# A gated-delta-rule scan in a two-layer hybrid kernel, rewritten so that each chunk takes one product and one addition

## The chip, the cores and the metric

The kernel runs on one core of a Trainium2 chip. The metric is the device time of one launch in microseconds (us). PE is TensorE (matrix products), PEld its weight loads, DVE is VectorE, ACT is ScalarE, POOL is GpSimd, SP is SyncE, which only issues DMAs here.

## The reference

There are 1024 tokens of width 1024 and two hybrid layers, followed by a second kind of block that the change doesn't touch. A hybrid layer projects its normed input to many columns, runs three mixers on them (GDN, a gated delta rule with 6 heads of 64; MLA, softmax attention with 6 heads; RWKV, a second recurrence with 4 heads), and projects their joined output back. GDN and RWKV run forwards and backwards over the tokens. GDN works in 16 chunks of 64 tokens; the change concerns its scan over the chunks:

```python
sol = lax.linalg.triangular_solve(a_mat, rhs, left_side=True, lower=True, unit_diagonal=True)
u0, w = sol[..., :dv], sol[..., dv:]
p_intra = jnp.einsum('nhcid,nhcjd->nhcij', q, k) * d_incl
q_g = q * gam[..., None]
k_d = k * jnp.exp(cum[..., -1:] - cum)[..., None]
g_end = jnp.exp(cum[..., -1])

def step(s, inp):
    w_c, u0_c, p_c, qg_c, kd_c, ge_c = inp
    u = u0_c - jnp.einsum('nhcd,nhde->nhce', w_c, s)
    o = jnp.einsum('nhcd,nhde->nhce', qg_c, s) + jnp.einsum('nhij,nhje->nhie', p_c, u)
    s = ge_c[..., None, None] * s + jnp.einsum('nhcd,nhce->nhde', kd_c, u)
    return s, o
```

## The kernel before

A hybrid layer has two stages. Stage A makes the input projection and, woven into it, GDN. Stage B runs MLA and RWKV woven together; after it comes the output projection.

The projections are the line L1036, here called dense: 128x512 products of high and low halves, 48 for an output tile, 27 tiles or 1,296 products in stage A of a layer and 384 for the output. In stage A, `paced` ties every second dense product to a tick on SP behind the products before, so that the scheduler spreads them among GDN's work. A dense product otherwise waits only for its weights (loaded by SP, split into high and low by ACT L996 and POOL L1000).

GDN takes its 6 heads in three pairs (head pairs 0, 1, 2), with the two directions on the two halves of the partitions. `gdn_front` of a pair is a generator in five phases: (1) convolution and norm of k and q on DVE (L192, L194); (2) convolution of v, transposes, decays; (3) the matrix `am` (L307); (4) the inverse of its diagonal blocks "by lanes" (L317, then 60 short DVE instructions L469 and L470), and the queries `q2` scaled by POOL (L327); (5) transposes back (L338, L341), the off-diagonal block (L350 to L361) and the products u (L375) and w (L380), evacuated by ACT (L366). `gdn_scan` then runs over the chunks of the pair. The text calls the scans S0, S1 and S2. In what order phases and scans are written is set by

```python
SEQ_A = "0 0 T3 1 1 1 0 1 S0 T3 2 2 2 1 2 S1 2 S2"
GDN_BUFS = dict(b8=5, b4=14, pad=2, fs=1, fx=2, gt=1, lan=1, xl=1, lt=1)
```

where a digit is the next phase of that pair, T3 three dense tiles, and GDN_BUFS says how many buffers each kind of tile has. `pt`, `am` and `q2` of a pair are the tiles of kind b8: five buffers for nine tiles in a layer. The two tiles of kind pad hold the input of a convolution, and also the factors `eg` by which `q2` is multiplied. `xt` is another name for `am`. Products that aren't dense use three PSUM banks (`k.ps`), the scan one (`k.pss`), its outputs another (`k.pso`).

A step of the scan before has two halves in a row: w times the state (`psw`, L419), subtracted from u by DVE (L421), then kd times u (`psk`, L427), added to the decayed state by two DVE instructions (L431). Each half is four 64x64 products (two heads, two directions).

Engines run their instructions in order; the order is fixed ahead, by a scheduler that looks at dependencies and buffers. In stage B the MLA products (scores L968, sums L921, values L931) are dealt out among RWKV's steps, which the text calls E0 to E3 (early parts), L0 to L3 (late parts) and scans; 1,146 MLA products in a layer.

Of the kernel before, what the change touches and what calls it, by code (L numbers as in the profile page):

```python
# [207 lines left out]
def gdn_front(k, hp, raw, prm, decays, eg_dram):  # L208
# [155 lines left out]

# [3 lines left out]
    last = None  # L368
    for b in range(4):
        pu, pw = (k.ps.tile([128, 512], F32, tag="mm", name=n("ps")) for _ in range(2))  # L370
        for j in range(8):
            nn = b * 8 + j
            for d in range(2):
                h = dh[d]
                nc.tensor.matmul(pu[h, j * 64 : j * 64 + 64], lhsT=xt[h, nn, :], rhs=vt(nn)[h], start=True, stop=True)  # L375
        done(pu, vt, b)
        for j in range(8):
            for d in range(2):
                h, m = dh[d], (b * 8 + j - 2) % 32
                nc.tensor.matmul(pw[h, j * 64 : j * 64 + 64], lhsT=gk(m)[h], rhs=xt[h, m, :], start=True, stop=True)  # L380
        if last is not None:
            done(last, gk, b - 1)
        last = pw
    done(last, gk, 3)
    yield dict(u=vt, wt=gk, kd=kd, pt=pt, qg=q2, ge=ge)


def gdn_scan(k, hp, F, prm, y_out):
# [3 lines left out]
    u, wt, kd, pt, qg, ge = (F[x] for x in ("u", "wt", "kd", "pt", "qg", "ge"))  # L392
    dh = [slice(0, 64), slice(64, 128)]
    z3 = lambda ps: ps[:, 0:128].rearrange("p (z e) -> p z e", e=CH)

    def outputs(d, half):
# [3 lines left out]
        for j in range(8):  # L400
            c = (half ^ d) * 8 + j
            sn = 15 - c if d else c
            for z in range(2):
# [3 lines left out]
                if sn:  # L407
                    nc.tensor.matmul(o, lhsT=wt(nn)[h], rhs=qg[h, z, c * 64 : c * 64 + 64], start=False, stop=True)
# [3 lines left out]
    for s in range(NST):  # L412

        after = (s + 1) % NST
        if s:
            psw = k.pss.tile([128, 512], F32, tag="sc", name=n("psw"))
            for h in dh:
                for z in range(2):
                    nc.tensor.matmul(psw[h, z * 64 : z * 64 + 64], lhsT=wt(2 * after + z)[h], rhs=wt(2 * s + z)[h], start=True, stop=True)  # L419
            x = u(2 * s, 2)  # L420
            nc.vector.tensor_tensor(x, x, z3(psw), op=ALU.subtract)  # L421
        if s < 15:
            psk = k.pss.tile([128, 512], F32, tag="sc", name=n("psk"))
            for h in dh:
                for z in range(2):
                    nn = 2 * s + z
                    nc.tensor.matmul(psk[h, z * 64 : z * 64 + 64], lhsT=kd(nn)[h], rhs=u(nn)[h], start=True, stop=True)  # L427
# [1418 lines left out]
```

## Time and profile before

| | |
|---|---|
| device time, median of 3 runs | 4023.65 us (4023.13 to 4024.43) |
| the profiled execution | 4012.39 us, of which the span is 4010.6 us |
| mean granted clock of PE in it | 0.903 of full speed |
| GDN's stage in layer 0, layer 1 | about 35 to 687 us, 1351 to 1985 us |
| second block, untouched | from about 2640 us |

Times inside the span are counted from its start. Busy shares are averages over the span; PE's busy time counts products that overlap in its pipeline with their full length.

### The profile page before, as it was taken

The numbers are of one execution on the slowest core, as the hardware profiler recorded it, in microseconds if no ns is written. First come the engines' busy times: TensorE is split into PE (matmuls) and PEld (weight loads), VectorE is DVE, ScalarE is ACT, GpSimd is POOL, SyncE is SP. The second block draws the span as 40 slices with busy tenths as digits, with TensorE's granted clock in tenths as the row PEclk, the third lists the DMA queues.
The fourth block names the chain that finished last, engine by engine and source line by source line (L and its number), as shares of the span: only waits on it lengthen the run. The fifth ranks groups of instructions, "written<-read, shape, count | busy, mean of one in ns | idle before, by whom it ended". The sixth has DMA issues, their size and how long they took to land. (4 is left out here: it accounts for less than half of the span.)

```text
span 4010.6 us, 70158 instructions
## 1 busy us (share of the span) xinstructions
PE 3444.1 (86%) x28908; PEld 2699.5 (67%) x28908; DVE 2360.2 (59%) x3270; ACT 1782.2 (44%) x2788; POOL 1373.0 (34%) x1367
## 2 busy tenths in 40 slices
PE   5878798798897877879879889779999998999898
PEld 4656665476675655557547667558898877887686
DVE  6695613866653468662485765358999975323223
ACT  6535236354452454423646445343344347555222
POOL 2432111351522243221244242333333445333361
PEclk9889799789888988889979979879999999999899
DMA  3322112000005232211200000411111111111432
GB/s 111 96 70 69 36 60 71 24 7 4 6 2 200 79 93 64 73 50 49 79 24 7 4 6 13 168 65 41 56 54 49 43 53 48 54 54 43 156 114 71
DMA packets 107073, 237.24 MB, mean 59 GB/s; under 512 B 13896, under 2 KB 16328, under 8 KB 106752
## 3 DMA queue, kind: packets, MB, share of 16 engines
q1 hardware_dynamic: 104000, 226.18, 17.3%
q8 instruction: 228, 3.74, 0.4%
q0 software_dynamic: 1024, 3.41, 0.3%
q10 hardware_dynamic: 1728, 3.15, 0.2%
q14 instruction: 93, 0.76, 0.1%
HBM read 164.17 MB, written 62.23 MB: 56 GB/s over the span
## 5 line engine op out<-in xcount | busy, mean ns | idle before, releaser
L1000 POOL TENSOR_TENSOR wl<-wr,wh 128x512 fp32r<-128x512 f32 x332 | 483.4, 1457 | 1421.8 <-ACT wh L996 1370.2
L1036 PE MATMUL psd<-hh,wh 128*128 128x512 f32 (+2 forms) x2272 | 901.6, 397 | 63.4 <-ACT pad L1425 20.7
L1036 PE MATMUL psd<-hl,wh 128*128 128x512 f32 (+2 forms) x2272 | 892.2, 393 | 41.1 <-DVE hl L1000 23.6
L1036 PE MATMUL psd<-hh,wl 128*128 128x512 f32 (+2 forms) x2272 | 888.8, 392 | 26.4 <-SPq L1092 23.2
L1036 PEld LDWEIGHTS psd<-hh,wh 128*128 128x128 f32 x2272 | 447.9, 197 | 160.3 <-ACT hh L996 23.5
L1036 PEld LDWEIGHTS psd<-hl,wh 128*128 128x128 f32 x2272 | 447.6, 197 | 128.1 <-DVE hl L1000 29.4
L1036 PEld LDWEIGHTS psd<-hh,wl 128*128 128x128 f32 x2272 | 449.1, 198 | 108.4 <-POOL wl L1000 19.1
L996 ACT ACTIVATE wh<-wr 128x512 fp32r<-128x512 f32 x332 | 208.2, 628 | 639.1 <-PE psd L1036 341.0
L1202 DVE SCALAR_TENSOR_TENSOR co<-pad,cw,co 128x1024 f32<-128x1024 f32 x240 | 364.6, 1519 | 5.8
L969 DVE TENSOR_REDUCE m<-pss 128x1 f32<-128x512 f32 x192 | 130.6, 686 | 103.8 <-PE pss L968 103.0
L923 ACT ACTIVATE ph<-ps 128x512 fp32r<-128x512 f32 x192 | 114.3, 595 | 170.9 <-PE pso L931 131.2
L924 DVE TENSOR_TENSOR pl<-ps,ph 128x512 fp32r<-128x512 f32 x192 | 131.7, 686 | 79.3 <-ACT ph L923 77.4
L1036 PE MATMUL psd<-hi,wh 128*128 128x512 f32 x384 | 149.8, 393 | 11.7 <-ACT wh L996 11.7
L973 ACT ACTIVATE p<-pss,m 128x512 f32<-128x512 f32 x192 | 130.0, 683 | 60.2 <-DVE m L970 50.1
L931 PE MATMUL pso<-pl,v 128*64 128x256 f32 x384 | 112.8, 328 | 50.8 <-DVE pl L924 50.4
L1036 PE MATMUL psd<-hi,wl 128*128 128x512 f32 x384 | 149.6, 392 | 5.3 <-POOL wl L1000 5.3
L1036 PE MATMUL psd<-lo,wh 128*128 128x512 f32 x384 | 150.1, 393 | 0.0
L469 POOL TENSOR_TENSOR lt<-lan,xl 64x30 f32<-64x30 f32 (+14 forms) x240 | 143.5, 598 | 17.4
L931 PE MATMUL pso<-ph,v 128*128 128x256 f32 x384 | 135.2, 357 | 16.4 <-ACT ph L923 10.5
L470 POOL TENSOR_TENSOR xl<-xl,lt 64x30 f32<-64x30 f32 (+14 forms) x240 | 142.8, 595 | 18.2
L1036 PE MATMUL psd<-mh,wh 128*128 128x512 f32 x256 | 101.8, 412 | 47.9 <-ACT wh L996 35.2
L921 PE MATMUL ps<-cst,p 128*128 128x128 f32 x768 | 140.5, 307 | 2.5 <-DVE v L904 2.5
(480 smaller groups left out, 7292.3 us busy)
## 6 DMA issues: line engine op xcount, KB each, us to landing
wr<-in_w_in SPq DMA_DIRECT2D x252, 256.0 KB, 2.6
proj<-st SPq DMA_DIRECT2D x108, 256.0 KB, 2.1
pad<-proj SPq DMA_DIRECT2D x32, 512.0 KB, 3.7
wr<-in_w_out SPq DMA_DIRECT2D x48, 256.0 KB, 2.7
y<-yd SPq DMA_DIRECT2D x16, 512.0 KB, 4.7
sg<-proj SPq DMA_DIRECT2D x16, 512.0 KB, 4.1
x<-x SPq DMA_DIRECT2D x16, 512.0 KB, 4.3
eg<-eg SPq DMA_DIRECT2D x24, 256.0 KB, 4.1
```

Of the source, the lines that this page charges most:

```text
L469: eng.tensor_tensor(t, a, b, op=ALU.mult)
L470: eng.tensor_tensor(x[:, j + 1 :, 0:j], x[:, j + 1 :, 0:j], t, op=ALU.subtract)
L921: yield nc.tensor.transpose(ps[:, c : c + 128], p[i][kt // 4][:, (kt % 4) * 128 : (kt % 4) * 128 + 128], k.c("ident"))
L923: nc.scalar.activation(ph, ps, AF.Copy)
L924: nc.vector.tensor_tensor(pl, ps, ph.bitcast(F32), op=ALU.subtract)
L931: yield nc.tensor.matmul(o, lhsT=l, rhs=r[:, c], start=kt + i == 0, stop=kt + i == 8)
L969: nc.vector.reduce_max(m[:, h : h + 1], pss[h], axis=AX.X)
L973: nc.scalar.activation(p[h], pss[h], AF.Exp, bias=m[:, 2:3], scale=SCALE, accum_out=sums[:, t, h : h + 1])
L996: first = nc.scalar.activation(hi, src, AF.Copy)
L1000: e.tensor_tensor(lo, src, hi.bitcast(F32), op=ALU.subtract)
L1036: yield nc.tensor.matmul(ps, lhsT=w(a)(i), rhs=x[b](i)[:, sl], start=i == 0 and a == b, stop=i == 7 and a == 1)
L1202: eng.scalar_tensor_tensor(out, pad[:, j : j + T], w[:, j : j + 1], out, op0=ALU.mult, op1=ALU.add)
```

## The change

Of the reference's step, u is put into the new state, which gives S to M S + C with M = g_end I − kd^T w and C = kd^T u0: both are known ahead of the scan. The output becomes (q_g − p w) S + p u0. So `gdn_front` phase 5 makes w and u with one loop (L373), then in four banks each M (POOL L380 makes g_end I, PE L386 the product, DVE L387 subtracts) and C (PE L386, ACT copy L365), then in four banks the corrected queries (PE L396, DVE L398 subtracts). `gdn_scan` has 14 steps of four products (L431) and one DVE addition (L433). M is written over `am` (`mt = xt`), C over `kd`, and the states grow in place of C. Lines of the changed kernel up to L460 differ from those before; below that they are one less (L1036 becomes L1035).

```diff
@@ -361,37 +361,50 @@
         nc.scalar.activation(xt[96:128, ns, 0:32], pv[96:128], AF.Copy)
 
 
-
     def done(ps, t, b):
         nc.scalar.activation(t(b * 8, 8), ps.rearrange("p (n d) -> p n d", d=CH), AF.Copy)
 
-    last = None
     for b in range(4):
-        pu, pw = (k.ps.tile([128, 512], F32, tag="mm", name=n("ps")) for _ in range(2))
-        for j in range(8):
-            nn = b * 8 + j
-            for d in range(2):
-                h = dh[d]
-                nc.tensor.matmul(pu[h, j * 64 : j * 64 + 64], lhsT=xt[h, nn, :], rhs=vt(nn)[h], start=True, stop=True)
-        done(pu, vt, b)
-        for j in range(8):
-            for d in range(2):
-                h, m = dh[d], (b * 8 + j - 2) % 32
-                nc.tensor.matmul(pw[h, j * 64 : j * 64 + 64], lhsT=gk(m)[h], rhs=xt[h, m, :], start=True, stop=True)
-        if last is not None:
-            done(last, gk, b - 1)
-        last = pw
-    done(last, gk, 3)
-    yield dict(u=vt, wt=gk, kd=kd, pt=pt, qg=q2, ge=ge)
+        for t in (gk, vt):
+            ps = k.ps.tile([128, 512], F32, tag="mm", name=n("ps"))
+            for j in range(8):
+                nn = b * 8 + j
+                for h in dh:
+                    nc.tensor.matmul(ps[h, j * 64 : j * 64 + 64], lhsT=xt[h, nn, :], rhs=t(nn)[h], start=True, stop=True)
+            done(ps, t, b)
+
+
+    mt = xt
+    for b in range(4):
+        ns = slice(b * 8, b * 8 + 8)
+        nc.gpsimd.tensor_tensor(mt[:, ns], k.c("eye2").unsqueeze(1).broadcast_to([128, 8, CH]), b3(ge[:, ns], CH), op=ALU.mult)
+        pm, pc = (k.ps.tile([128, 512], F32, tag="mm", name=n("ps")) for _ in range(2))
+        for ps, l, r in ((pm, gk, kd), (pc, kd, vt)):
+            for j in range(8):
+                nn = b * 8 + j
+                for h in dh:
+                    nc.tensor.matmul(ps[h, j * 64 : j * 64 + 64], lhsT=l(nn)[h], rhs=r(nn)[h], start=True, stop=True)
+        nc.vector.tensor_tensor(mt[:, ns], mt[:, ns], pm.rearrange("p (n d) -> p n d", d=CH), op=ALU.subtract)
+        done(pc, kd, b)
+    for b in range(4):
+        ps = k.ps.tile([128, 2, 4, CH], F32, tag="mm", name=n("ps"))
+        for j in range(4):
+            for z in range(2):
+                for d, h in enumerate(dh):
+                    c = b * 4 + j
+                    nn = 2 * (15 - c if d else c) + z
+                    nc.tensor.matmul(ps[h, z, j], lhsT=gk(nn)[h], rhs=pt[h, nn, :], start=True, stop=True)
+        x = q2[:, :, b * 256 : b * 256 + 256]
+        nc.vector.tensor_tensor(x, x, ps.rearrange("p z c i -> p z (c i)"), op=ALU.subtract)
+    yield dict(u=vt, m=mt, st=kd, pt=pt, qg=q2)
 
 
 def gdn_scan(k, hp, F, prm, y_out):
 
     nc, g = k.nc, k.g
     n = k.name
-    u, wt, kd, pt, qg, ge = (F[x] for x in ("u", "wt", "kd", "pt", "qg", "ge"))
+    u, m, st, pt, qg = (F[x] for x in ("u", "m", "st", "pt", "qg"))
     dh = [slice(0, 64), slice(64, 128)]
-    z3 = lambda ps: ps[:, 0:128].rearrange("p (z e) -> p z e", e=CH)
 
     def outputs(d, half):
 
@@ -405,34 +418,20 @@
                 o = ps[dh[z], j * 64 : j * 64 + 64]
                 nc.tensor.matmul(o, lhsT=u(nn)[h], rhs=pt[h, nn, :], start=True, stop=sn == 0)
                 if sn:
-                    nc.tensor.matmul(o, lhsT=wt(nn)[h], rhs=qg[h, z, c * 64 : c * 64 + 64], start=False, stop=True)
+                    nc.tensor.matmul(o, lhsT=st(nn - 2)[h], rhs=qg[h, z, c * 64 : c * 64 + 64], start=False, stop=True)
         return ps
 
     y = []
-    for s in range(NST):
-
-        after = (s + 1) % NST
-        if s:
-            psw = k.pss.tile([128, 512], F32, tag="sc", name=n("psw"))
+
+    for s in range(1, NST - 1):
+        psk = k.pss.tile([128, 512], F32, tag="sc", name=n("psk"))
+        for z in range(2):
             for h in dh:
-                for z in range(2):
-                    nc.tensor.matmul(psw[h, z * 64 : z * 64 + 64], lhsT=wt(2 * after + z)[h], rhs=wt(2 * s + z)[h], start=True, stop=True)
-            x = u(2 * s, 2)
-            nc.vector.tensor_tensor(x, x, z3(psw), op=ALU.subtract)
-        if s < 15:
-            psk = k.pss.tile([128, 512], F32, tag="sc", name=n("psk"))
-            for h in dh:
-                for z in range(2):
-                    nn = 2 * s + z
-                    nc.tensor.matmul(psk[h, z * 64 : z * 64 + 64], lhsT=kd(nn)[h], rhs=u(nn)[h], start=True, stop=True)
-            if s:
-                for z in range(2):
-                    nn = 2 * s + z
-                    nc.vector.scalar_tensor_tensor(
-                        wt(nn + 2), wt(nn), ge[:, nn : nn + 1], psk[:, z * 64 : z * 64 + 64], op0=ALU.mult, op1=ALU.add)
-            else:
-                nc.vector.tensor_copy(wt(2, 2), z3(psk))
-        if s in (9, 11):
+                nn = 2 * s + z
+                nc.tensor.matmul(psk[h, z * 64 : z * 64 + 64], lhsT=m[h, nn, :], rhs=st(nn - 2)[h], start=True, stop=True)
+        x = st(2 * s, 2)
+        nc.vector.tensor_tensor(x, x, psk[:, 0:128].rearrange("p (z e) -> p z e", e=CH), op=ALU.add)
+        if s in (8, 10):
             y.append(g.tile([128, 512], F32, tag="fx", name=n("y")))
             nc.scalar.activation(y[-1], outputs(len(y) - 1, 0), AF.Copy)
     for d in range(2):
```

Counted over the program, PE has 20,984 products in place of 20,216 (128 more for each of the six head pairs), DVE 3,112 in place of 3,244 instructions, POOL 24 more, ACT 58 more, SP as many as before.

The first place is PE in S0 of layer 0: a step before, with its two sets of products (`psw`, `psk`) and dense (`psd`) and output products (`pso`) between them,

```order
L419 MATMUL psw_1937<-gk_742 64x64 x4
L1036 MATMUL psd_4339<-hl_230,wh_4265 128x512
L1036 MATMUL psd_4339<-hh_229,wl_4266 128x512
L1036 MATMUL psd_4339<-hh_229,wh_4314 128x512
L1036 MATMUL psd_4339<-hl_230,wh_4314 128x512
L427 MATMUL psk_1943<-vt_748,kd_722 64x64 x4
L406 MATMUL pso_2042<-pt_768,vt_748 64x64
L408 MATMUL pso_2042<-q_220_996,gk_742 64x64
```

and a step of the changed kernel there:

```order
L431 MATMUL psk_2150<-kd_722,am_797 64x64 x4
L421 MATMUL pso_2187<-q_220_996,kd_722 64x64
L419 MATMUL pso_2187<-pt_768,vt_748 64x64
L421 MATMUL pso_2187<-q_220_996,kd_722 64x64
L419 MATMUL pso_2187<-pt_768,vt_748 64x64
L1035 MATMUL psd_4669<-hh_229,wl_4596 128x512
L1035 MATMUL psd_4669<-hh_229,wh_4595 128x512
L1035 MATMUL psd_4669<-hl_230,wh_4595 128x512
L1035 MATMUL psd_4669<-hh_229,wl_4596 128x512
L431 MATMUL psk_2156<-kd_722,am_797 64x64 x4
```

Where eight dense products and two sets of scan products made a step, there are now four dense products, four output products and one set.

The second place is DVE in S0 of layer 0. Before, the steps of S0 (`vt`, `gk`), the lane inverse of head pair 1 (`lt`, `xl`) and the convolutions of head pair 2 (`k_404`, `q_405`, from `pad`) alternate:

```order
L470 TENSOR_TENSOR xl_1812<-xl_1812,lt_1875 128x10x21
L421 TENSOR_TENSOR vt_748<-vt_748,psw_1950 128x128
L194 SCALAR_TENSOR_TENSOR q_405_2539<-pad_2550,prm_174,q_405_2539 128x1024
L194 SCALAR_TENSOR_TENSOR k_404_2538<-pad_2540,prm_174,k_404_2538 128x1024
L469 TENSOR_TENSOR lt_1878<-lan_1807,xl_1812 128x198
L431 SCALAR_TENSOR_TENSOR gk_742<-gk_742,ex_699,psk_1956 128x64 x2
L194 SCALAR_TENSOR_TENSOR q_405_2539<-pad_2550,prm_174,q_405_2539 128x1024
L194 SCALAR_TENSOR_TENSOR k_404_2538<-pad_2540,prm_174,k_404_2538 128x1024
L470 TENSOR_TENSOR xl_1812<-xl_1812,lt_1878 128x9x22
L421 TENSOR_TENSOR vt_748<-vt_748,psw_1963 128x128
```

In the changed kernel DVE has the whole lane inverse of pair 1 first, then the subtractions L387 and L398 of pair 0, then 14 additions of S0 in a row; its last two, and the convolutions of pair 2 behind them:

```order
L433 TENSOR_TENSOR kd_723<-kd_723,psk_2276 128x128
L433 TENSOR_TENSOR kd_723<-kd_723,psk_2282 128x128
L438 TENSOR_TENSOR y_2231<-y_2231,pso_2288 128x512
L192 TENSOR_SCALAR k_400_2648<-pad_2650,prm_174 128x1024
L194 SCALAR_TENSOR_TENSOR k_400_2648<-pad_2650,prm_174,k_400_2648 128x1024 x2
L192 TENSOR_SCALAR q_401_2649<-pad_2660,prm_174 128x1024
L438 TENSOR_TENSOR y_2186<-y_2186,pso_2322 128x512
```

`M` in the buffer of `am` lives until S0 ends, so the `q2` of pair 1 has no buffer of kind b8 until then. On POOL its two products with `eg` stand after the four L380 of pair 0, and the tiles of kind pad that hold `eg` come free for the convolutions of pair 2 behind them.

The third place is PE near the end of stage A of layer 0, at the dense product number 1,200 of 1,296. Before, dense products with few others:

```order
L1036 MATMUL psd_5535<-hh_229,wh_5461 128x512
L1036 MATMUL psd_5535<-hl_230,wh_5461 128x512
L877 MATMUL ps_5797<-sq_5794,cst_58 128x512
L1036 MATMUL psd_5535<-hh_229,wl_5462 128x512
L1036 MATMUL psd_5535<-hh_229,wh_5461 128x512
L1036 MATMUL psd_5535<-hl_230,wh_5461 128x512
L1036 MATMUL psd_5535<-hh_229,wl_5462 128x512
L1036 MATMUL psd_5535<-hh_229,wh_5461 128x512
```

In the changed kernel the products of MLA (L930, L967, L920, of lines one less than before) stand among them:

```order
L1035 MATMUL psd_5819<-hl_230,wh_5748 128x512
L1035 MATMUL psd_5819<-hh_229,wl_5749 128x512
L1035 MATMUL psd_5865<-hh_229,wh_5791 128x512
L1035 MATMUL psd_5865<-hl_230,wh_5791 128x512
L930 MATMUL pso_7125<-ph_7175,v_6165 128x256
L1035 MATMUL psd_5865<-hh_229,wl_5792 128x512
L1035 MATMUL psd_5865<-hh_229,wh_5791 128x512
L967 MATMUL pss_7220<-kh_6097,qh_6099 128x512
L967 MATMUL pss_7220<-kl_6098,qh_6099 128x512
L967 MATMUL pss_7220<-kh_6097,ql_6100 128x512
L930 MATMUL pso_7125<-pl_7176,v_6165 64x256
L930 MATMUL pso_7125<-ph_7175,v_6165 128x256
```

Counted in PE's order of layer 0: ahead of the last output of S2 there stood 1,106 dense products and now 882; by the end of the norm that follows it, 1,122 and now 898; at the last dense product 79 products of MLA had been issued and now 406. From there to RWKV's step E3 there stand 1,708 PE instructions and now 1,680. Behind E3 to the end of stage B there were 1,096, 299 of them of MLA, and now 797, none of MLA. In layer 1 at the end of GDN 2,816 dense products of both layers had been issued and now 2,592 of the 2,976; at the last of them 44 products of MLA and now 380.

## Rows read from the trace of the kernel before

**Rows 1.** The page, busy time of each engine, with its share of the span.
```profile
PE 3444.1 (86%) x28908; PEld 2699.5 (67%) x28908; DVE 2360.2 (59%) x3270; ACT 1782.2 (44%) x2788; POOL 1373.0 (34%) x1367
```

**Rows 2.** Stages of layer 0: length, busy time (instructions) by engine, clock, DMA.
```profile
597.00:687.00 90.00, 74.35 (x279) 49.37 (x278) 30.95 (x51) 58.53 (x81) 19.12 (x20) 0.92 0.19 63
687.00:1069.00 382.00, 320.39 (x2593) 229.80 (x2591) 273.92 (x420) 176.01 (x342) 149.71 (x228) 0.81 0.05 17
1069.00:1227.00 158.00, 138.60 (x1803) 110.47 (x1801) 79.06 (x143) 87.05 (x162) 41.80 (x71) 0.89 0.10 35
```

**Rows 3.** Timeline of POOL, layers 0 and 1: start, length, line, operation, [idle before].
```profile
597.30 0.69 POOL L858 DMA_DIRECT2D mc<-cs  x1
...
687.15 0.96 POOL L90 MEMSET rm<- 128x1024 bf16 x1 [13.94 <-PE psd L1036]
...
1922.93 0.56 POOL L858 DMA_DIRECT2D mc<-cs  x1
...
1985.87 0.96 POOL L90 MEMSET rm<- 128x1024 bf16 x1
```

**Rows 4.** Line L1036 alone in stretches of layer 0: PE busy, PEld busy, clock, DMA.
```profile
268.00:374.00 106.00, 54.12 (x176) 33.65 (x174) 0.87 0.24 72
...
489.00:597.00 108.00, 64.47 (x216) 37.62 (x216) 0.98 0.15 50
597.00:655.00 58.00, 33.07 (x111) 22.36 (x109) 0.88 0.26 84
663.00:687.00 24.00, 14.19 (x48) 8.00 (x47) 1.00 0.06 23
```

**Rows 5.** Timeline of PE and DVE, one step of the scan of head pair 2.
```profile
549.27 0.46 PE L419 MATMUL psw<-gk 64*64 64x64 f32 x8
...
549.78 0.29 DVE L421 TENSOR_TENSOR vt<-vt,psw 128x128 f32<-128x128 f32 x1 [1.31 <-PE psw L419]
...
550.22 0.40 PE L1036 MATMUL psd<-hl,wh 128*128 128x512 f32 x1
...
550.45 0.40 PE L1036 MATMUL psd<-hh,wl 128*128 128x512 f32 x1
...
552.56 0.46 PE L419 MATMUL psw<-gk 64*64 64x64 f32 x8
```

**Rows 6.** Timeline of PE, a bank of 64x64 products ahead of the scan.
```profile
276.52 1.10 PE L375 MATMUL ps<-vt,am 64*64 64x64 f32 x32
```

**Rows 7.** Timeline of POOL at head pair 1's queries.
```profile
288.75 4.82 POOL L327 TENSOR_TENSOR q<-q,eg 128x1024 f32<-128x1024 f32 x2 [8.12 <-DMA q<-q]
```

**Rows 8.** Timeline of DVE, layer 0, head pairs 0 to 2.
```profile
280.44 0.21 DVE L469 TENSOR_TENSOR lt<-lan,xl 128x30 f32<-128x30 f32 x1 [0.80 <-ACT xl L462]
...
376.34 0.69 DVE L439 TENSOR_TENSOR y<-y,pso 128x512 f32<-128x512 f32 x1 [2.27 <-PE pso L408]
...
429.53 8.12 DVE L317 STREAM_TRANSPOSE lan<-am 32x1024 f32<-32x1024 f32 x4 [8.92 <-PE ps L358]
438.77 0.20 DVE L469 TENSOR_TENSOR lt<-lan,xl 128x30 f32<-128x30 f32 x1 [1.12 <-ACT xl L462]
...
466.56 2.00 DVE L338 STREAM_TRANSPOSE am<-xl 32x1024 f32<-32x1024 f32 x1
```

**Rows 9.** Timeline of PE, MLA's smaller products in a row.
```profile
700.87 0.40 PE L931 MATMUL pso<-pl,v 128*64 128x256 f32 x2
...
701.23 0.60 PE L921 MATMUL ps<-cst,p 128*128 128x128 f32 x4
```

**Rows 10.** Line L968 alone (MLA's scores) in three stretches.
```profile
597.00:655.00 58.00, 0.00 (x0) 0.12 (x1) 0.88 0.26 84
663.00:687.00 24.00, 5.40 (x19) 3.62 (x20) 1.00 0.06 23
687.00:1069.00 382.00, 69.48 (x192) 37.73 (x191) 0.81 0.05 17
```

**Rows 11.** Timeline of DVE, RWKV's scan with MLA finished.
```profile
1206.29 0.22 DVE L751 TENSOR_TENSOR kb<-kb,psg 128x64 f32<-128x64 f32 x1 [0.58 <-PE psg L750]
```

## The prediction

> **What bounds the kernel now.** I read the page's busy times first, and don't take them as they stand: PE is at 86%, but its weight loads, which run beside the products, are at 67% [rows 1], and in an undisturbed stretch one dense product starts 0.23 us behind the other while each counts 0.40 us [rows 5]. So PE has slack, and the question is which chain holds each stage. The reader takes that from POOL's timeline [rows 3]. MLA's first instruction (L858) is issued at 597.30 in layer 0, when GDN has ended (the end of S2 with its outputs and norm; I read 593). RWKV's first (L90) is issued at 687.15, having waited 13.94 us for a dense product, the last of the 1,296. So there are two gates in a layer: the end of GDN opens MLA, the end of dense opens RWKV. In layer 1 the same two instructions stand at 1922.93 (GDN ends at about 1910) and 1985.87.
>
> Then the stages [rows 2]: 90 us with dense and the start of MLA (597 to 687), 382 us with RWKV and MLA woven (687 to 1069, up to E3), and 158 us behind it. RWKV lies behind the last dense product, so whatever moves that product moves the layer's end, less what RWKV gains by having fewer MLA products among its own.
>
> Dense runs in GDN's shadow: 176 products in 106 us of S0's time, 216 in 108 us of S2's [rows 4]. At 0.23 us each they fill a third to a half of it. GDN's time is thus no pure loss, and a shorter GDN pushes dense out behind it. The order (front part) says by how much: of 1,296 dense products 1,122 stood ahead of the end of GDN, now 898.
>
> **The change part by part.**
>
> *A scan step.* In S2 one step took 3.29 us, from one L419 to the next [rows 5]; the DVE subtraction is 0.29 us, and it had waited 1.31 us. The new step has four dense products (0.92 us) and one set of scan products (0.46 us with its tail): 1.4 us. Fourteen of these are 20 us, where 15 of 3.29 were 49.
>
> *Work added ahead of the scan.* 128 map products, 64 of the queries. A bank of 16 products (32 records) takes 1.10 us [rows 6], of which I count the last 0.17 as pipeline, so 12 banks at 0.93 are 11 us of PE; what the scan loses is 64 of its 124 products, 3.7 us. The net is 7.4 us a pair, 22 us a layer, 44 us in all. Of DVE, eight 128x512 passes out of PSUM; the like L439 takes 0.69 us [rows 8], 5.5 us a pair. The removed are 15 subtractions and 28 short L431, about 12 us. With three PSUM banks for all of this and ACT copies between, u, w, maps and queries of a pair should take about 24 banks x 0.93 = 22 us, less what of them lies inside the phase before.
>
> *The first scan, S0.* The order on DVE puts the maps' last subtractions behind the whole lane inverse of pair 1 (from 280.44; another pair's took 27.8 us, from 438.77 to 466.56), two more subtractions (1.4) and the transposes back (five or six of 2.00 us) [rows 8]: 318 to 320, with the four subtractions of the queries 323. PE has no dense product in its queue there, so it stands still for some 36 us. Then 14 steps, 20 us, and the rest of the outputs, 12 us: S0 ends at about 355, before at 376 [rows 8]. A gain of 21 us.
>
> *The buffer that is held.* M lives in `am`, so the queries of pair 1 wait for S0's end; before they were scaled by POOL at 288.75 [rows 7], 4.82 us for the two, and the `pad` tiles came free for pair 2's convolutions, which DVE did inside S0. Now: DMA of q2 4 us, POOL 4.8, load of pad 3.6, convolutions and norm of k and q 20, v 11, `am` of pair 2 14, then the off-diagonal blocks of pair 1: about 417. The lane transposes of pair 2 stood at 429.53, having waited 8.92 us [rows 8]: 12 of the 21 us are kept. Transposes 8, lane inverse 27.8 as now (438.77 to 466.56 [rows 8]), transposes 11: 466. S1 follows with 21 us, then u to queries of pair 2 (to 512) and S2 with outputs and norm, 30 us: GDN ends at about **543 instead of 593**. I take the same 50 us for layer 1: 1860 instead of 1910. Bounds: 30 if evacuations with three banks are slow, 70 if pair 2's convolutions are not late.
>
> *What then waits.* At 543 there are 398 dense products left, with 406 of MLA among them. MLA needs its start-up first: no score product in the 58 us after 597, with 111 dense [rows 4, 10]. Taken with its loads as 68 us and 152 dense products, that is 611. Then 246 dense products mixed with 366 of MLA, which come in units of 12 L968, 16 L931 and 16 L921 (44). PE alone could do dense and L968 at 0.23 us, L931 at 0.12, L921 at 0.11 [rows 5, 9]: 246 x 0.23 + 366 x 0.145 = 109 us. The only stretch that has both shows 48 dense and 19 L968 (1.6 units) in 24 us [rows 4, 10], 15.2 us a unit; but its L931 lag, and by all three lines there were 1.1 units, 21.6 us each. The 8.3 units are 127 us by the first, 180 by the second. I take 135, nearer to the first, since MLA's softmax has no RWKV beside it. Dense ends at 611 + 135 = 746 instead of 687: **+59**. Layer 1: 384 dense products left at 1860; 68 us; then 232 dense with 346 of MLA, 127 us: 2055 instead of 1985, **+70**.
>
> *What comes back.* From there to E3 PE's order has 28 instructions fewer out of 1,708, and 740 of MLA for 768: the 382 us stay, less 8. Behind E3 no MLA is left, where 299 of it lay before. PE was busy 138.60 of 158 us there [rows 2]; 299 x 0.145 = 43 us of that goes, but the bare chain shows too: a scan step of RWKV with no MLA beside it takes 0.22 + 0.58 = 0.80 us [rows 11], PE waiting for DVE in each, and the last scan can't start before POOL has ended a lane inverse. I take 32 us off (20 to 52). Together **−40**.
>
> *The sum*, on the profiled execution: layer 0 +59 − 40 = +19, layer 1 +70 − 40 = +30; 4012.4 + 49 = 4061. The median of three stood 11 us over the profiled execution, so **4073 us**. Everything from the end of stage B on is the same.
>
> **The rivals.**
>
> *Faster: the mix runs at PE's own rate.* If dense and MLA go at PE's 109 us (layer 1: 103), dense ends at 720 and 2031, +33 and +46. If RWKV's end then shrinks by 52 and 8, the layers give −27 and −14: 4012 − 41 = 3971, 3982 as a median. For it: PE's order has a dense product ready in each gap of MLA, and the MLA rate in 663 to 687 with full clock. Against: L931 waits for ACT and DVE there, and granted clock was 0.81 in the next stage [rows 2]. It decides from a mix of about 115 us down. A shorter start-up of MLA works the same way.
>
> *Cancelled: +40 and +45 at the gates, −40 each behind.* 4012 + 5, 4028 as a median at most; within 0.2% (8 us; a measurement of this kernel can't tell less from no change) from 4016 to 4032.
>
> *Only PE counts.* If PE were full throughout, as its 86% suggests, the 44 us of products would be added and all moves cancel: 4012 + 44 = 4056, 4068 as a median. That is nearly the forecast's time by another way; the end of GDN tells the two apart (about 593, or 543). Against it stand the weight loads at 67% and the 0.23 us between products that count 0.40 [rows 1, 5]. The Trainium skill, Perfetto Trace Analysis, section Identifying the Most-Contended Engine, says so as a rule: a matmul's busy time is a poor measure of how full TensorE is, since matmuls are pipelined, and the weight loads' share a better one. By that rule a third of PE's time is free and the 44 us could vanish in it, which leaves 4012 and 4023 as a median if nothing else moved. The trace agrees with the rule (67 against 86%), and the forecast keeps to the gates.
>
> *Worse: MLA's chain holds dense.* In 382 us with RWKV there were 192 L968 [rows 10], 16 units, 23.9 us each. At 20 us a unit the mixes are 167 and 157 us, dense ends at 778 and 2085, +91 and +100, and with −34 behind: +57, +66, 4135, 4146 as a median. Since PE runs in order, each dense product behind a waiting L931 waits with it. Against: DVE and ACT have less to do without RWKV.
>
> **How the numbers follow.** Forecast (4045 to 4105) 0.42; worse 0.12; only PE 0.06: slower 0.60 with these. Faster 0.28, its times from 3960 to 4015. Cancelled 0.12. The range of 8 in 10 reaches from the faster rival's middle to between forecast and worse: 3980 to 4125.
>
> **What would show it.** In the new trace: 14 L433 about 1.4 us apart; L380 to L398 of S0 done by 323 and PE idle before; pair 2's convolutions behind 355; L858 at about 547 and L90 at about 746; 366 MLA products between; no L968 behind E3. It would be wrong if L90 comes before 715 (the mix is at PE's rate), if L858 comes later than 575 (the banks or the held buffer cost more), or if the stage from L90 to the end of RWKV, 540 us before, loses less than 25 or more than 55.

## The result and the profile after

The changed kernel takes **4173.59 us** (median of 4 runs, 4169.02 to 4176.44) against 4023.39 us before: ratio 1.0378 (95% interval 1.0359 to 1.0396), 150 us slower. The forecast was 4073, its range ended at 4125. The direction was right, the size was a third of what came. The page of the profiled execution (4175.31 us):

```profile
span 4173.5 us, 73097 instructions
...
PE 3496.3 (84%) x30444; PEld 2784.7 (67%) x30444; DVE 2351.4 (56%) x3138; ACT 1838.9 (44%) x2846; POOL 1409.0 (34%) x1391
```

PE's share and that of its weight loads (84 and 67%) are about those of before [rows 1]; nothing in them tells of 150 us. POOL's timeline does, with the two gates of each layer, MLA's first instruction (L857) and RWKV's first (L90), as in [rows 3]:

```profile
593.82 0.69 POOL L857 DMA_DIRECT2D mc<-cs  x1
...
788.67 0.96 POOL L90 MEMSET rm<- 128x1024 bf16 x1 [13.72 <-PE psd L1035]
...
1985.28 0.56 POOL L857 DMA_DIRECT2D mc<-cs  x1
...
2174.98 0.96 POOL L90 MEMSET rm<- 128x1024 bf16 x1 [5.83 <-PE psd L1035]
```

In layer 0 MLA opens 3.5 us earlier (593.82 for 597.30), RWKV 101.5 us later (788.67 for 687.15), still behind a dense product. L857 (L858 before) marks the end of GDN only roughly, since it also waits behind a weight split in POOL's order: before, it came 7 us ahead of GDN's last norm, here 2 us behind it. From there to the output projection 526 us pass, before 551: 76 us lost. In layer 1 it is 84 us by the same reading, and the two make the difference of the spans, 163 us, to 3 us. Where dense went, line L1035 alone (length, PE busy, PEld busy, clock, DMA), as in [rows 4]:

```profile
268.00:328.00 60.00, 3.68 (x14) 2.39 (x14) 0.74 0.04 11
328.00:457.00 129.00, 72.82 (x239) 47.64 (x238) 0.89 0.24 72
457.00:510.00 53.00, 1.07 (x5) 0.57 (x4) 0.74 0.02 7
510.00:592.00 82.00, 27.95 (x97) 16.53 (x95) 0.98 0.14 44
592.00:789.00 197.00, 111.84 (x380) 67.81 (x380) 0.98 0.16 54
```

In two stretches of 60 and 53 us stand 14 and 5 dense products; before, 176 stood in the 106 us from 268 on. Behind GDN there are 380 in 197 us. In the two stretches PE waits in its own order; two banks of S0, in the timeline of PE:

```profile
300.95 1.97 PE L386 MATMUL ps<-vt,kd 64*64 64x64 f32 x32 [9.73 <-DVE am L387]
...
320.77 5.94 PE L396 MATMUL ps<-pt,gk 64*64 64x64 f32 x126 [11.86 <-DVE am L387]
```

The wait of 11.86 us is for the last subtractions L387, behind DVE's lane inverse, as forecast (320.77 for 318 to 323). The timeline of DVE has the convolutions and the matrix `am` of pair 2, its lane transposes, and two scan steps of S2, as in [rows 5, 8]; below it the first and last product of `pt` on POOL:

```profile
361.06 0.75 DVE L192 TENSOR_SCALAR k<-pad,prm 128x1024 f32<-128x1024 f32 x1 [8.36 <-DMA pad<-proj]
...
433.68 0.42 DVE L307 TENSOR_TENSOR am<-ps,pt 64x256 f32<-64x256 f32 x1 [25.89 <-POOL gt L283]
...
455.09 1.97 DVE L317 STREAM_TRANSPOSE lan<-am 32x1024 f32<-32x1024 f32 x1 [6.18 <-PE ps L358]
...
565.61 0.29 DVE L433 TENSOR_TENSOR kd<-kd,psk 128x128 f32<-128x128 f32 x1 [1.45 <-PE psk L431]
566.69 0.29 DVE L433 TENSOR_TENSOR kd<-kd,psk 128x128 f32<-128x128 f32 x1 [0.80 <-PE psk L431]
```

```profile
416.50 1.28 POOL L284 TENSOR_TENSOR pt<-pt,gt 128x512 f32<-128x512 f32 x1 [4.49 <-ACT pt L282]
...
433.69 1.27 POOL L284 TENSOR_TENSOR pt<-pt,gt 128x512 f32<-128x512 f32 x1
```

The scan steps of S2 stand 1.1 to 2.3 us apart (1.7 us on the mean of 14, 1.4 forecast, 3.29 before). Pair 2's lane transposes come at 455.09, forecast 417, before 429.53: `am` had waited 25.89 us for POOL, which makes the decays of pair 2 (L279 to L284, up to 433.69 + 1.27) among the splits of dense weights. At last the stages behind GDN as in [rows 2], MLA's scores L967 as in [rows 10] and a bare step of RWKV's scan as in [rows 11]:

```profile
592.00:789.00 197.00, 177.68 (x822) 128.28 (x822) 87.97 (x150) 129.01 (x209) 38.14 (x35) 0.98 0.16 54
789.00:1171.00 382.00, 315.14 (x2641) 232.76 (x2639) 272.39 (x409) 179.60 (x344) 153.65 (x229) 0.81 0.08 28
1171.00:1314.00 143.00, 98.54 (x1416) 83.03 (x1414) 30.22 (x65) 43.64 (x68) 31.78 (x65) 0.65 0.08 30
```

```profile
592.00:789.00 197.00, 32.34 (x108) 19.27 (x108) 0.98 0.16 54
789.00:1171.00 382.00, 68.43 (x180) 37.91 (x180) 0.81 0.08 28
1171.00:1303.00 132.00, 0.00 (x0) 0.00 (x0) 0.66 0.02 7
```

```profile
1285.94 0.22 DVE L750 TENSOR_TENSOR kb<-kb,psg 128x64 f32<-128x64 f32 x1 [0.58 <-PE psg L749]
```

108 of the layer's 288 score products now stand ahead of the gate, none behind 1171. RWKV's bare step is the same 0.80 us. The last stretch takes 143 us up to the first output product, with PE at a granted clock of 0.65; before, the 169 us from 1069 up to that product had 0.87, the 158 us up to RWKV's end 0.89.

### The profile page after: what moved, and what is told of

It reads as the page before. It is cut to its first block, busy times and chain, and to the rows that moved or that the text cites. A ratio compares the mean times of both kernels' runs of the same rounds, so it can differ in the third digit from the quotient of the medians.

```text
span 4173.5 us, 73097 instructions
## 1 busy us (share of the span) xinstructions
PE 3496.3 (84%) x30444; PEld 2784.7 (67%) x30444; DVE 2351.4 (56%) x3138; ACT 1838.9 (44%) x2846; POOL 1409.0 (34%) x1391
## 5 line engine op out<-in xcount | busy, mean ns | idle before, releaser
L999 POOL TENSOR_TENSOR wl<-wr,wh 128x512 fp32r<-128x512 f32 x332 | 492.5, 1485 | 1520.6 <-ACT wh L995 1450.3
L1035 PE MATMUL psd<-hh,wh 128*128 128x512 f32 (+2 forms) x2272 | 895.2, 394 | 68.1 <-ACT pad L1424 21.5
L1035 PE MATMUL psd<-hl,wh 128*128 128x512 f32 (+2 forms) x2272 | 888.6, 391 | 52.9 <-SPq L1091 25.6
L1035 PE MATMUL psd<-hh,wl 128*128 128x512 f32 (+2 forms) x2272 | 881.6, 388 | 17.3 <-SPq L1091 13.6
L1035 PEld LDWEIGHTS psd<-hh,wh 128*128 128x128 f32 x2272 | 446.2, 196 | 163.9 <-ACT pad L1424 22.6
L1035 PEld LDWEIGHTS psd<-hl,wh 128*128 128x128 f32 x2272 | 445.5, 196 | 145.4 <-SPq L1091 35.3
L1035 PEld LDWEIGHTS psd<-hh,wl 128*128 128x128 f32 x2272 | 446.7, 197 | 100.1 <-issue 15.5
L968 DVE TENSOR_REDUCE m<-pss 128x1 f32<-128x512 f32 x192 | 130.6, 687 | 112.1 <-PE pss L967 111.0
L930 PE MATMUL pso<-pl,v 128*64 128x256 f32 x384 | 109.4, 319 | 63.7 <-DVE pl L923 63.2
L1035 PE MATMUL psd<-hi,wh 128*128 128x512 f32 x384 | 149.8, 394 | 11.7 <-ACT wh L995 11.7
L1035 PE MATMUL psd<-hi,wl 128*128 128x512 f32 x384 | 149.6, 393 | 5.3 <-POOL wl L999 5.3
L1035 PE MATMUL psd<-lo,wh 128*128 128x512 f32 x384 | 150.0, 393 | 0.0
L930 PE MATMUL pso<-ph,v 128*128 128x256 f32 x384 | 128.1, 337 | 23.4 <-ACT ph L922 12.0
L1035 PE MATMUL psd<-mh,wh 128*128 128x512 f32 x256 | 101.1, 409 | 47.9 <-ACT wh L995 34.2
L920 PE MATMUL ps<-cst,p 128*128 128x128 f32 x768 | 138.0, 304 | 1.0 <-DVE v L903 1.0
```

What stands on the lines that cost most here:

```text
L920: yield nc.tensor.transpose(ps[:, c : c + 128], p[i][kt // 4][:, (kt % 4) * 128 : (kt % 4) * 128 + 128], k.c("ident"))
L930: yield nc.tensor.matmul(o, lhsT=l, rhs=r[:, c], start=kt + i == 0, stop=kt + i == 8)
L968: nc.vector.reduce_max(m[:, h : h + 1], pss[h], axis=AX.X)
L999: e.tensor_tensor(lo, src, hi.bitcast(F32), op=ALU.subtract)
L1035: yield nc.tensor.matmul(ps, lhsT=w(a)(i), rhs=x[b](i)[:, sl], start=i == 0 and a == b, stop=i == 7 and a == 1)
```

## The experiments

All times stand against the kernel before on the same chip, which there took 4008 to 4015 us, where beside the changed kernel it took 4023. Each diff shows only its telling lines. Theory H is the held buffer, S and W (later W2) are PE's waits for banks and its added products, Q and R are that PE's work and its standing still count wherever they lie; P, G and G2 all mean the place of dense in PE's order, and grew out of one another: a dense product pushed behind GDN lies among MLA's, and RWKV waits for the last one.

**b_hold.** The kernel before with `am` held through the scan:

```diff
+    nc.vector.tensor_tensor(held, F["am"][:, 0, 0:1], y[1][:, 0:1], op=ALU.add)
```

> The kernel before, with one tiny addition at the end of each scan that reads the buffer am, so that am is held through the scan as the change holds it; nothing else is added. Theory H (the held buffer: the queries of pair 1 and the convolutions of pair 2 come only after S0) expects the lane inverse of pair 2 to start about 25 us later than at 439, GDN to end 20 to 30 us later in each layer, and 4060 to 4090 us. Theory P (what counts is how many dense products stand under GDN in PE's order, since each that is pushed behind it costs about 0.5 us among MLA's) looks at the order: 1216 dense products now stand ahead of S2's last output, where 1106 did, so the last dense product comes hardly later and the time is 4015 to 4050 us.

4009.95 us, ratio 0.9987 (0.9964 to 1.0011): no change. Its gates in layer 0:

```profile
639.31 0.69 POOL L860 DMA_DIRECT2D mc<-cs  x1
...
655.58 0.96 POOL L90 MEMSET rm<- 128x1024 bf16 x1 [3.51 <-PE psd L1038]
```

GDN ends 33 us later than before, a little more than H expects, and the last dense product comes 32 us *earlier*, since more dense lay under the longer GDN (42 products left at its end, 162 before). H has fallen for this kernel: a later end of GDN cost nothing here, with more dense done under it. P's lower bound for the time was 5 us too high.

**m_in_gk.** The changed kernel with the queries corrected ahead of the maps and M over `gk`:

```diff
-        nc.vector.tensor_tensor(mt[:, ns], mt[:, ns], pm.rearrange("p (n d) -> p n d", d=CH), op=ALU.subtract)
+        nc.vector.tensor_tensor(gk(b * 8, 8), gt, pm.rearrange("p (n d) -> p n d", d=CH), op=ALU.subtract)
```

> The changed kernel, but the queries are corrected ahead of the maps and M is written over w (gk) instead of am, by way of the tile gt. am comes free before the scan as in the kernel before; pair 2's convolutions stand in pair 1's lane inverse again. Theory H expects GDN to end at 550 to 560 instead of 592 and the kernel to gain the same 30 to 40 us a layer: 4095 to 4115. Theory P expects GDN's end earlier too, but in PE's order only 800 dense products stand ahead of it (882 in the changed kernel), so the last one stays at 780 to 800 and the time at 4150 to 4190.

4171.25 us (1.0401, 1.0371 to 1.0432), as P said:

```profile
568.24 0.71 POOL L858 DMA_DIRECT2D mc<-cs  x1
...
801.11 0.96 POOL L90 MEMSET rm<- 128x1024 bf16 x1
```

GDN ends 27 us earlier than in the changed kernel, and the gate comes 12 us later, since 460 dense products are left instead of 380.

**m_by_act.** Map banks evacuated by ACT:

```diff
+        nc.scalar.activation(mt[:, ns], pm.rearrange("p (n d) -> p n d", d=CH), AF.Copy, scale=-1.0)
+        nc.gpsimd.tensor_tensor(mt[:, ns], mt[:, ns], gt, op=ALU.add)
```

> The changed kernel with the map banks taken out of PSUM by ACT (a copy with factor -1) and g_end I added by POOL, so that no map bank waits for DVE; PE's order has the same counts of dense products. Theory S (PE stands still because the banks wait for DVE's lane inverse) expects the two gaps of 52 us without dense products to shrink by 10 to 20 us each, GDN to end 30 us earlier, and 4110 to 4130. Theory P expects the queries' subtractions to hold PE at the same place, the last dense product within 10 us of 789, and 4160 to 4185.

4215.77 us (1.0512, 1.0482 to 1.0543). S expected a gain and has fallen: the stretches without dense stay (52, 56 and 36 us). P was right in that, but its time was 31 us too small and its gate too early: GDN ends 19 us later than in the changed kernel, the last dense product 18 us later, at 806.5, where P had allowed 10. Why GDN ends later was not looked into.

**b_dummy.** The kernel before with 128 products a pair thrown away:

```diff
+                nc.tensor.matmul(ps[h, j * 64 : j * 64 + 64], lhsT=kd(b * 4)[h], rhs=vt(b * 4)[h], start=True, stop=True)
```

> The kernel before with 128 more 64x64 products a pair behind u and w, in eight banks that ACT reads one column of; their results are thrown away, and everything that the reference asks for is computed. Theory W (only the added PE work costs) expects 22 us a layer: 4060 to 4070. Theory P looks at the order, where 1006 dense products stand ahead of S2's last output instead of 1106 and 206 MLA products ahead of the last dense one instead of 59: 100 x 0.49 us less what RWKV gets back, 30 to 40 us a layer beside 7 us a pair of scan delay: 4085 to 4130.

4148.38 us (1.0344, 1.0314 to 1.0374). Above both: 137 us for 44 us of products. The gate is at 750, 258 dense products are left at GDN's end (162 before), and layer 1 loses more than layer 0.

**fr10, ff8, ff12, unpaced_end** keep all maps and move dense: written behind the banks of phase 5 (fr10), tied between them (ff8, ff12), or freed of SP's pacing behind S2.

```diff
             done(ps, t, b)
+            k.fill(10)
```

> The changed kernel with 10 dense products written, unpaced, behind each bank of u and w and 20 behind each pair of map banks. The scheduler moves them ahead, so PE's order has 1088 of 1296 dense products ahead of S2's last output (882 in the changed kernel, 1106 before) and 70 MLA products ahead of the last dense one (364; before 59), but phase 5 still stands in runs of 300 to 445 instructions without a dense one. Theory G (the gates of the forecast: the last dense product opens RWKV, all else hangs on it) expects it near 690 to 720 in layer 0 and 4030 to 4075. Theory Q (PE is the bound: a layer takes PE's work plus the time that PE stands still in its own queue, wherever that is; the changed kernel has 22 us more work, about 29 us more standing still in phase 5 and 19 us more behind the last dense product, where MLA's products no longer fill RWKV's waits) expects only the last part back: 4115 to 4150.

4030.01 us (1.0037, 1.0016 to 1.0057): 135 of the 150 us are back, each kernel against the kernel before on its own chip, though the stretches without dense are still 50, 59 and 36 us long and no product was taken out. Q has fallen, G stands. The gates:

```profile
617.58 0.69 POOL L859 DMA_DIRECT2D mc<-cs  x1
...
700.67 0.96 POOL L90 MEMSET rm<- 128x1024 bf16 x1 [15.63 <-PE psd L1037]
```

> The changed kernel with 8 dense products tied into PE's order between any two banks of phase 5 (16 behind a pair of map banks). In the order 1016 dense products stand ahead of S2's last output and 169 MLA products ahead of the last dense one. Theory Q expects the standing still in phase 5 to go (about 29 us a layer) and half of the part behind the last dense product: 4075 to 4120. Theory G expects the scans to come later by the dense products put ahead of their banks, GDN to end at 620 or later, and no gain: 4140 to 4180.

4192.67 us (1.0439, 1.0383 to 1.0494): the tie holds dense back ahead of phase 5 (96 us without a dense product from 168 on), GDN ends at 654, the gate is at 777. Both misjudged the size. Whether filling PE's waits inside phase 5 buys anything is not shown by this run, because the tie moves dense away elsewhere.

> The same with 12 dense products between two banks (24 behind a pair of map banks): 1256 dense products ahead of S2's last output, no MLA product ahead of the last dense one, and the longest run of phase 5 without a dense one 289 instructions. Theory Q expects 22 us of work a layer to be left and at most 10 us of standing still: 4050 to 4085. Theory G expects GDN and the last dense product to end near 700 to 720: 4080 to 4130.

4105.38 us (1.0221, 1.0170 to 1.0273), within G's bounds, 20 us above Q's: GDN's end at 691 and the gate at 694, a little ahead of G's 700 to 720.

> The changed kernel with the dense products that are written behind S2 taken out of the pacing by SP. The scheduler then fills the scans with them: 1296 of 1296 stand ahead of S2's last output, none among MLA's, but phase 5's runs without a dense product (363 to 487 instructions) stay, and S2's phase 5 has none left. Theory G expects the last dense product near GDN's end, 650 to 690, and 4010 to 4060. Theory Q expects the tail's 19 us back and the standing still in phase 5 kept or grown: 4110 to 4150.

4034.96 us (1.0074, 1.0044 to 1.0103), G again in the time; dense has ended at 637 (650 to 690 expected), GDN at 666. RWKV's L90 is issued at 637.10, 0.5 us behind the last dense product and 29 us ahead of GDN's end, so it is dense that opens it.

**mla_after.** The changed kernel, MLA's scores tied behind the last dense product:

```diff
+                                if k.last_dense is not None:
+                                    k.tc.add_manual_dep(ins.ins, k.last_dense.ins.name, SYNC, reason="scores behind dense")
```

> The changed kernel, but MLA's first score product may only start behind the last dense product of the layer's stage A. PE's order is that of the changed kernel up to GDN's end (882 dense products ahead of S2's last output), then the rest of dense with no attention product among it (364 in the changed kernel). Theory G2 (an attention product ahead of the last dense one holds the gate back by 0.3 us, 109 us for 364, and RWKV's stage gives back 0.1 us for each, since it waits for its own chain) expects the last dense product at 685 to 705 in layer 0, 570 to 590 us from there to the output projection, and 4080 to 4115. Theory R (PE does the same work in any case; what it does of MLA earlier it needn't do later) expects 4160 to 4185.

4093.76 us (1.0223, 1.0163 to 1.0283; two runs, 26 us apart). By doing MLA later it lies 85 us above the kernel before on its chip, where the changed kernel lay 150 above it: about 65 us came back (80 between the two medians). R has fallen. The gates, and the dense line from GDN's end to the gate:

```profile
599.48 0.69 POOL L857 DMA_DIRECT2D mc<-cs  x1
...
716.14 0.96 POOL L90 MEMSET rm<- 128x1024 bf16 x1 [11.45 <-PE psd L1039]
```

```profile
598.00:716.00 118.00, 96.72 (x380) 71.25 (x380) 0.96 0.26 86
```

The same 380 dense products take 118 us in place of 197. So 364 attention products among them cost 79 us, 0.22 each (0.3 expected). From the gate to the output projection it takes 559 us, 33 more than with them done ahead: 0.09 each. The gate came 11 us behind G2's bounds and the 559 us are 11 under them; the time is within.

**b_late.** The kernel before, its GDN unchanged, dense from number 898 on tied behind S2:

```diff
-                    run(steps)
+                    run(itertools.islice(steps, 898 - 480))
+                    ins = next(steps)
+                    k.tc.add_manual_dep(ins.ins, k.s2_end.ins.name, SYNC, reason="dense behind S2")
+                    run(steps)
```

> The kernel before with nothing changed in GDN: the dense products behind number 898 of a layer may only start behind S2, as many as stand there in the changed kernel, and 371 attention products then stand ahead of the last one (364 in the changed kernel). Theory G2 (where dense stands is the cause) expects GDN's end at 585 to 600, the last dense product at 780 to 800, 520 to 530 us behind it, and 4140 to 4180, nearly the whole loss without a map being made. Theory W2 (the maps, their products and PE's standing still for them are the cause) expects 4010 to 4050.

**4172.55 us** (1.0411, 1.0385 to 1.0437): the loss of the changed kernel without one of its maps, 163 us where that lost 150. G2 stands and W2 has fallen. Its gates, and line L1036 in S2's time and behind it, beside [rows 4]:

```profile
588.69 0.69 POOL L858 DMA_DIRECT2D mc<-cs  x1
...
788.44 0.96 POOL L90 MEMSET rm<- 128x1024 bf16 x1
```

```profile
489.00:597.00 108.00, 13.12 (x34) 9.71 (x35) 0.62 0.09 30
597.00:790.00 193.00, 107.29 (x366) 62.33 (x364) 1.00 0.13 46
```

**b_dummy_fr** (bfr20, below, with b_dummy's products):

> bfr20 with the 128 added products a pair of b_dummy, whose results are thrown away: 1120 dense products ahead of S2's last output, 24 attention products ahead of the last dense one. Theory G2 expects what the counts say, the last dense product at 670 to 700 and 545 to 570 us behind it: 3995 to 4040, so that of b_dummy's 137 us 110 or more were the place of dense. Theory W2 expects b_dummy's loss on top of bfr20: 4090 to 4130.

4031.61 us (1.0054, 1.0035 to 1.0073). With dense put forward the thrown-away products cost 47 us (1.0054 beside bfr20's 0.9936) where they had cost 137: W2's sum of losses has fallen. The 47 us are near the 44 that were counted for the products, but they aren't their price alone, since dense moved too: 142 dense products are left at GDN's end (18 in bfr20), and the gate comes 55 us later.

**bfr20, xfr10, xfr14**: dense written unpaced into phase 5 of the kernel before (20 behind each bank of w), and of m_in_gk (10 and 14).

> A control: the kernel before with dense products written unpaced in phase 5 (20 behind each bank of w), so that 1242 stand ahead of S2's last output and no attention product ahead of the last dense one. If writing dense into phase 5 is a gain of its own (fr10 was 143 us faster than the changed kernel), it should show here too: 3880 to 3930. Theory G2 expects what b_hold showed with about the same counts (1216 and 0): the gate 30 us earlier, RWKV's stage 25 us longer, 4000 to 4030.

**3982.88 us, ratio 0.9936 (0.9916 to 0.9955)**: faster than both kernels. The control gains 26 us where fr10 gained 135, so most of fr10's gain is the change's own loss undone. It beats G2's bounds by 17 us, with the gate 59 us earlier (30 expected) and 42 us more behind it (25):

```profile
607.25 0.69 POOL L859 DMA_DIRECT2D mc<-cs  x1 [1.18 <-PE pso L409]
...
628.47 0.96 POOL L90 MEMSET rm<- 128x1024 bf16 x1 [14.30 <-PE psd L1037]
```

> M written over w (as in m_in_gk) together with dense written unpaced into phase 5 (as in fr10): 1018 dense products ahead of S2's last output, 169 attention products ahead of the last dense one. Theory G2 expects GDN's end at 585 to 600, the last dense product at 700 to 720 and 530 to 540 us behind it: 4020 to 4070. If the held buffer costs once dense is placed well, it is faster than fr10 (4030), 3990 to 4015.

4050.99 us (1.0123, 1.0074 to 1.0172), as G2 said, not faster than fr10.

> The same with 14 and 28 dense products: 1208 ahead of S2's last output, no attention product ahead of the last dense one. Theory G2 expects the last dense product at 640 to 665 and 570 to 585 us behind it, 4000 to 4040; theory R, that PE's work counts, expects no difference to xfr10.

4005.88 us (0.9996, 0.9978 to 1.0014): the best version with maps equals the kernel before, and is 23 us above bfr20. It is 45 us under xfr10 with the same work on PE, so R has fallen here too.

Layer 0 of twelve kernels, read from the traces (us; dense products left at the norm that ends GDN; attention products ahead of the last dense one, counted in PE's order by the lines of scores, sums and values):

| kernel | GDN's end | dense left | attention ahead | last dense | from there to output projection | output projection |
|---|---|---|---|---|---|---|
| before | 604 | 162 | 59 | 687 | 551 | 1238 |
| changed | 592 | 380 | 364 | 788 | 526 | 1314 |
| b_late | 587 | 386 | 371 | 787 | 518 | 1305 |
| m_in_gk | 565 | 460 | 452 | 799 | 516 | 1314 |
| b_dummy | 615 | 258 | 206 | 750 | 546 | 1296 |
| b_dummy_fr | 618 | 142 | 24 | 683 | 555 | 1238 |
| fr10 | 611 | 184 | 70 | 700 | 534 | 1234 |
| mla_after | 598 | 380 | 0 | 716 | 559 | 1274 |
| b_hold | 637 | 42 | 0 | 655 | 574 | 1229 |
| ff12 | 691 | 11 | 0 | 694 | 585 | 1279 |
| xfr14 | 637 | 56 | 0 | 658 | 574 | 1231 |
| bfr20 | 618 | 18 | 0 | 628 | 593 | 1221 |

## Why the prediction was wrong

The mechanism was right: the last dense product opens RWKV, dense is pushed out from under GDN, and MLA done ahead gives back less than it costs. b_late shows it alone, mla_after shows the price. Two terms of the sum were mis-sized.

**GDN ends at 543 instead of 593** is the step that failed most: the changed kernel's GDN ended at 592. The forecast's own sign for this came true, L857 at 593.82 and so later than 575. In DVE's timeline, the last addition of outputs and the last norm of S2 before, and the last norm in the changed kernel:

```profile
592.81 0.69 DVE L439 TENSOR_TENSOR y<-y,pso 128x512 f32<-128x512 f32 x1 [2.88 <-PE pso L408]
...
604.15 0.75 DVE L452 SCALAR_TENSOR_TENSOR sq<-y,prm,sq 128x512 f32<-128x512 f32 x1 [3.28 <-ACT sq L451]
```

```profile
592.00 0.75 DVE L451 SCALAR_TENSOR_TENSOR sq<-y,prm,sq 128x512 f32<-128x512 f32 x1 [3.28 <-ACT sq L450]
```

So the 593 that I read for GDN's end before was the last output; with the norm, which the 543 includes, it was 604. Read alike, GDN became 12 us shorter, not 50. And though it was only 12 us shorter, 380 dense products were left at its end, where 162 had been: PE's order put them there, not the shorter time.

S0 came nearly as worked out: queries corrected by 327 (forecast 323), the last output at 365.04 (355), because DVE's order has it behind the first of pair 2's convolutions, which began at 361.06. Behind it the chain of pair 2 left out one phase: the decays that POOL makes between convolution and `am`, for which DVE waited 25.89 us. The convolutions and norms took 47 us (361.06 to 407.79), not 31, with waits for ACT in them, though they began 6 us sooner than counted. So the lane transposes came at 455.09, not 417. S2 with outputs and norm took 39 us (553.58 to 592.75), not 30: the steps took 1.7 us, not 1.4, and outputs and norm 16 us, not 10.

With a gate at GDN's end plus 203 us (68 + 135), that moved the gate from 746 to 795; 196 us came, 7 less than forecast. MLA's start-up was shorter (51 us and 102 dense products, up to the first L967 at 643.47; 68 and 152 forecast), and the mix of the other 278 with 364 of MLA took 145 us, 1.24 times what PE alone would need at the forecast's prices, as in the forecast (135 for 109). The gate was 101.5 us late where +59 had been said; 113 in layer 1 (+70).

**What comes back, −40,** was 25 us and 29 us. The part up to E3 came as said: POOL's L630, at 1162.5, stands 374 us behind the gate, where L631 stood 382 before. Behind E3, −32 had been taken and −17 came, from 169 to 152 us. PE waits for RWKV's own chain there, which doesn't get shorter with MLA gone, and PE runs at a lower granted clock. fr10 still has as many PE records behind E3 as the kernel before, 306 more than the changed kernel, and took 164 us there at a granted clock of 0.89, against 0.67: taking them away gave 12 us. How much of the missing 15 us is the clock's was not measured by itself.

So per layer +76 and +84 came, not +19 and +30. Of the miss in layer 0, 57 us, the later end of GDN makes 49, the shorter way from there to the gate −7, and what didn't come back 15. Two small slips changed nothing: the scan had 120 products, not 124 (64 of them went), and the sum for S0's maps gives 320 to 322, not 318 to 320.

What the runs add is that the end of GDN doesn't tell the time by itself. In b_hold GDN ended 33 us later at no cost, in m_in_gk 27 us sooner than in the changed kernel at no gain: where the dense products lie decides.

*The rivals.* "Worse" had the right size (4146) by a dearer mix (20 us a unit); the mix was not dearer, it began later. "Only PE counts" fell with fr10, mla_after and b_late, though the added products do cost something: at most 47 us in b_dummy_fr. The Trainium skill, Perfetto Trace Analysis, section Identifying the Most-Contended Engine, calls matmul busy time a poor measure of how close TensorE is to its roofline; the trace agrees, since PE's share fell from 86 to 84% while 150 us were lost. That the products could vanish in PE's free third, which I drew from it, was not borne out: b_dummy lost 137 us with dense moved by them, b_dummy_fr 47. "Faster" needed 183 us from GDN's end to the gate (68 + 115); 196 came, and GDN's end was late.

*The order against the trace.* What I called 36 us of standing still in S0 was there (52 us with few dense products).

What stays open: why writing dense into phase 5 moves it so far ahead in the order while tying it there (ff8) does the reverse is a matter of the scheduler, which wasn't looked into; and layer 1's extra loss in b_dummy was not traced.

## What to carry to other kernels

In a stage where two streams share PE, a shorter chain is no gain by itself: count which work of the other stream stood in its waits, where the order puts that work now, and what waits for its last instruction. Before costing a new algorithm, hold the old one and move only the bystander (b_late, one dependency): here that gave the whole loss. And try the placement by itself: here it was worth 26 us (0.6%) without the change.

## What the runs showed of the hardware

Where RWKV ran without MLA beside it the mean granted clock was lower: 0.65 of full speed from 1171 to 1314 in the changed kernel, with PE busy 98.54 of 143 us, against 0.89 from 1069 to 1227 before, 138.60 of 158 [rows 2]. These are means of two levels, 0.50 and 1.00 (1.2 and 2.4 GHz). In these kernels it goes with the missing MLA work and not with the maps: b_late, which makes no map, has 0.65 there (1153 to 1305, PE busy 107.16 of 152), and fr10, which makes them all, 0.89 (1071 to 1234, 133.22 of 163). The mean of the span went from 0.903 to 0.887, and to 0.914 in fr10.

RWKV's bare scan step feels the level, although it took 0.80 us in both kernels: it stood at 0.50 in both (1204 to 1210 before, 1283 to 1290 in the changed kernel). At 1.00 (1271 to 1276.6 in the changed kernel) PE's four products of a step took 0.33 us instead of 0.48, and one such step 0.65:

```profile
1274.21 0.22 DVE L750 TENSOR_TENSOR kb<-kb,psg 128x64 f32<-128x64 f32 x1 [0.65 <-PE psg L749]
...
1274.48 0.33 PE L749 MATMUL psg<-kb,rk 64*64 64x64 f32 x4 [0.32 <-DVE kb L750]
1274.86 0.22 DVE L750 TENSOR_TENSOR kb<-kb,psg 128x64 f32<-128x64 f32 x1 [0.43 <-PE psg L749]
...
1285.41 0.48 PE L749 MATMUL psg<-kb,rk 64*64 64x64 f32 x4 [0.32 <-DVE kb L750]
```

The 0.80 us by which the forecast priced the bare chain [rows 11] was thus a price at the lower level.
